# Down projection of a two-layer encoder trunk: the running sums of its weight blocks, added by GpSimd or added by the DMA engines while they load

## The chip, the cores and the metric

The kernel runs on one core of one Trainium2 chip. The metric is the device time of one execution in microseconds, as the median of several runs. Profiles are taken by the hardware profiler from one further execution. The core has TensorE (PE; its weight loads are listed as PEld), VectorE (DVE), ScalarE (ACT), GpSimd (POOL) and SyncE (SP), each with a queue of its own that it works through in order, and sixteen DMA engines that carry the transfers that SP, ACT and POOL issue.

## What is computed

Two batches (512 and 256 tokens, 1024 features) go through a trunk of two layers with shared weights: attention, then a squared-ReLU MLP, each added to the residual stream. Only the last part matters here, once in each layer:

```python
h = rmsnorm(x, ln_mlp[layer])
x = x + jnp.square(jax.nn.relu(h @ w_up[layer])) @ w_down[layer]
```

`w_up` is 1024 x 4096 and `w_down` 4096 x 1024. After the second layer a final RMSNorm gives the output.

## The kernel before

All 768 tokens are kept together, features on the 128 partitions. A product in float32 is made of three passes of reduced precision: each operand is split into a high half and a low half (ACT copies the high half, `whi` or the first plane of `th`; DVE subtracts it to get the low half, `wlo` or the second plane of `th`), and PE adds high x high, high x low and low x high.

Both MLP products are done as 2 x 2 blocks with a scheme of seven block products in place of eight. In such a scheme the operands of the products are sums and differences of the blocks. For the up projection the weights' sums are made on POOL (line 843). The hidden activations, squared, and the differences of them that the down projection needs, go out to DRAM (tensor `T`: ACT's queue stores z, line 879, POOL's queue stores t, line 887) and come back later.

The down projection (from line 953) works through 28 steps in each layer: seven products in the order 1, 2, 7, 4, 5, 6, 3, and in each the four groups `i` of hidden features. A step multiplies 48 times: four banks of 384 columns (`dn`, line 1019), four slices each, three passes each. Its weights are two tiles of 128 x 1024 (`rp` 0 and 1); the first serves the first two banks, the second the last two, so I call the work on one tile a half-step. The weights of a product are:

- product 1: block 11 as loaded; product 7: that tile plus block 21 ("the chain's tile": what product 1 used is added to)
- product 2: block 12 alone
- product 4: block 22, loaded afresh; product 5: that plus block 21; product 6: that plus block 11; product 3: that plus block 12

The host has arranged blocks and signs so that only additions are left. Eight chain tiles are alive (`kept[i, rp]`), and each is split into `whi` and `wlo` (four buffers each) for every product that uses it, then changed in place by the next sum, four steps later (eight steps between products 1 and 7).

Three helpers order the work around step `s`. `fetch(s + 3)` issues the loads of a step's two weight tiles from SP (line 978). They go to `ch` (8 buffers, the chain's tiles), to `wd` (6 buffers) or, every third of the others, to `wraw` (3 buffers, shared with the other stages), as do the two first tiles of all. `sums(s + 2)` adds the loaded block onto the chain's tile on POOL (line 985). `halves(s + 1)` splits (lines 80 and 81). `operand(s + 2)` loads the activations `tr` from `T` through SP (line 911; 768 KB) and splits them into `th` (lines 116 and 117). The framework places all semaphores and plans the order on each engine's queue by its own expected times, so that loads can be issued earlier than the source has them.

At the end of each product DVE adds the banks into the residual x (line 865 through `fold`), ACT evacuates product 1's banks into `u` (line 1025). In layer 1 the final norm is worked in between the last steps (lines 1075 to 1091). When a stage begins, the tiles `ch`, `wd` and `acs` take the places of the up projection's tiles, so their first loads wait until these are free.

Of the kernel before, what the change touches and what calls it, by code (L numbers as in the profile page):

```python
# [11 lines left out]
F32 = mybir.dt.float32  # L12
F32R = mybir.dt.float32r
AF = mybir.ActivationFunctionType
ALU = mybir.AluOpType
AX = mybir.AxisListType

P = 128
# [19 lines left out]
def kernel(ctx: ExitStack, tc: tile.TileContext, a: dict, y: bass.AP):  # L38
    nc = tc.nc
# [3 lines left out]
    wpool = ctx.enter_context(tc.tile_pool(name="wpool", bufs=1))  # L43
# [17 lines left out]
    def ps_tile(tag, name):  # L61
        return psum.tile([P, 512], F32, tag=tag, name=name, bufs=BANKS[tag])
# [706 lines left out]
    def mlp(layer, src, o, x, es):  # L769
# [50 lines left out]
        def weights(plain=False):  # L820


            raws = []
            for _ in range(2):
                raw, loads = wload("w_up", 1024)
                loads[0]()
                raws.append(raw)
            a11, a22, a12, a21 = (r[:, i * 512 : (i + 1) * 512] for r in raws for i in range(2))
            if plain:
                out = {}  # L830
                for t, ij in zip(raws, (((0, 0), (1, 1)), ((0, 1), (1, 0)))):
                    hi, lo = whilo(1024)
                    wsplit(hi, lo, t)
                    for i, b in enumerate(ij):
                        out[b] = (hi, lo), i * 512
                return out
            sa, sb = (up.tile([P, 1024], F32, tag="s", name="s", bufs=3) for _ in range(2))
            s2, s1, s3, s4 = (r[:, i * 512 : (i + 1) * 512] for r in (sa, sb) for i in range(2))
            out = {}
            for ps_, t in (((1, 4), raws[0]), ((6, 5), sa), ((7, 3), sb), ((2,), raws[1])):  # L840
                if t is sa:
                    for d_, x_, y_ in ((s1, a21, a22), (s2, s1, a11), (s3, a11, a21), (s4, a12, s2)):
                        nc.gpsimd.tensor_tensor(out=d_, in0=x_, in1=y_, op=ALU.add)  # L843
                w = 512 * len(ps_)
                hi, lo = whilo(w)
                wsplit(hi, lo, t[:, :w])
                for i, p in enumerate(ps_):
                    out[p] = (hi, lo), i * 512
            return out
# [58 lines left out]
        def operand(n, i):  # L908

            tr = pa_.tile([P, ND, HT], F32, tag="tr", name="tr", bufs=2)  # L910
            nc.sync.dma_start(tr, T[i][:, SLOT[n]])
            th = pa_.tile([P, 2, ND, HT], F32R, tag="th", name="th", bufs=3)
            halve(th[:, 0], th[:, 1], tr)
            return th

        for mp in range(2, FF // 256):
            w = weights()
# [35 lines left out]
        acs = st.enter_context(tc.tile_pool(name="acs", bufs=1, reuse_waits="tile"))  # L953
        wds = ExitStack()
        ch = wds.enter_context(tc.tile_pool(name="ch", bufs=8, side="right", reuse_waits="tile"))
        wd = wds.enter_context(tc.tile_pool(name="wd", bufs=6, side="right", reuse_waits="tile"))
        u = acs.tile([P, 4, HT], F32, name=f"u_{layer}")
        PR = (0, 1)
        ORDER = (1, 2, 7, 4, 5, 6, 3)
# [1 line left out]
        BLOCK = {1: 11, 2: 12, 7: 21, 4: 22, 5: 21, 6: 11, 3: 12}  # L961
        steps = [(n, i) for n in ORDER for i in range(NG)]
        kept, new, parts = {}, {}, {}
        third = [0]

        def fetch(n, i):

            for rp in PR:
                off = (((layer * NG + i) * 4 + (11, 22, 21, 12).index(BLOCK[n])) * 2 + rp) * P * 1024
                if n in (1, 4) and (n, i) != (1, 0):  # L970
                    t = ch.tile([P, 1024], F32, tag="ch", name="ch", bufs=8)
                else:
                    third[0] += n != 1
                    if n == 1 or third[0] % 3 == 0:
                        t = wpool.tile([P, 1024], F32, tag="wraw", name="wd", bufs=3)
                    else:
                        t = wd.tile([P, 1024], F32, tag="wd", name="wd", bufs=6)
                nc.sync.dma_start(t, a["w_down"][off : off + P * 1024].rearrange("(p w) -> p w", w=1024))
                (kept if n in (1, 4) else new)[i, rp] = t

        def sums(n, i):
            for rp in PR:
                if n in (7, 5, 6, 3):
                    t = kept[i, rp]
                    nc.gpsimd.tensor_tensor(out=t, in0=t, in1=new.pop((i, rp)), op=ALU.add)  # L985

        def halves(n, i):
            for rp in PR:
                hi, lo = whilo(1024)
                wsplit(hi, lo, new.pop((i, rp)) if n == 2 else kept[i, rp])  # L990
                parts[n, i, rp] = hi, lo

        def fold(out, x_, op=ALU.add):
            add(out, out, x_, op)
# [7 lines left out]
        for s, (n, i) in enumerate(steps):  # L1002
            if s + 3 < len(steps):
                fetch(*steps[s + 3])
            if s + 2 < len(steps):
                sums(*steps[s + 2])
                ths.append(operand(*steps[s + 2]))
            if s + 1 < len(steps):
                halves(*steps[s + 1])
            if i == 0:  # L1010
                odd = ORDER.index(n) % 2
                banks = [ps_tile("at" if odd or r == 3 else "mm", "dn")[:, :HT] for r in range(4)]
            th = ths.pop(0)
            for r, ps in enumerate(banks):
                w = parts[n, i, r // 2]
                for q in range(ND):
                    c = (r % 2) * 512 + q * P
                    for k, (a_, b_) in enumerate(((0, 0), (0, 1), (1, 0))):
                        nc.tensor.matmul(ps, w[a_][:, c : c + P], th[:, b_, q],  # L1019
                                         start=i + q + k == 0, stop=i == NG - 1 and q == ND - 1 and k == 2)  # L1020
            if i == NG - 1:
                for r, ps in enumerate(banks):
                    x12, x11, x22, x21 = (xb(r, m_, sl) for m_ in PR for sl in (A, B))
                    if n == 1:
                        nc.scalar.activation(u[:, r], ps, AF.Copy)
                    if n in (1, 2):
                        fold(x11, ps)
                    if n == 4:
                        fold(x21, ps)
                    if n in (7, 5):  # L1030
                        fold(x22, ps, ALU.subtract)
                    if n == 7:
                        fold(x21, ps, ALU.subtract)
                    if n in (5, 3):
                        fold(x12, ps)
                    if n == 6:
                        fold(u[:, r], ps)
                        fold(x21, u[:, r], ALU.subtract)
                        fold(x22, u[:, r], ALU.subtract)
                        fold(x12, u[:, r])  # L1040
            if layer == 1 and n == 3 and i < NG - 1:
                last[0](i)
            elif layer == 1 and n == 6 and i == NG - 1:
                last = [final(x, lambda: acs.tile([P, HT], F32, tag="sq", name="sq", bufs=4), s_) for s_ in (HT, 0)]
# [18 lines left out]
    def final(x, sq, s):  # L1063

        acc = cpool.tile([P, NT], F32, tag="acc", name="acc", bufs=1) if s else accs[0]
        R = cpool.tile([P, NT], F32, tag="R", name="R", bufs=1) if s else accs[1]
        accs[:] = [acc, R]
        ms = (0, 2, 4, 6, 1, 3, 5, 7) if s else (1, 3, 5, 7, 0, 2, 4, 6)
        sl = slice(s, s + HT)
        nm = Norm(None, (s, s + HT), acc)  # L1070
        rt = []

        def part(i):
            if i == 0:
                nc.scalar.activation(acc[:, sl], x[ms[0]][:, sl], AF.Square)
                nm.parts = [acc[:, sl]]
                for n, m in enumerate(ms[1:]):
                    t = sq()
                    nc.scalar.activation(t, x[m][:, sl], AF.Square)
                    if n < 5:  # L1080
                        nc.vector.tensor_tensor(out=acc[:, sl], in0=acc[:, sl], in1=t, op=ALU.add)
                    else:
                        nm.parts.append(t)
            elif i == 1:
                rt.append(nm.rstd(s))
            else:
                nm.spread(rt[0], R)
                for k in ms:
                    yt = x[k][:, sl]
                    nc.vector.scalar_tensor_tensor(out=yt, in0=yt, scalar=gcol(G_F, k), in1=R[:, sl], op0=ALU.mult, op1=ALU.mult)  # L1090
                    (nc.sync, nc.scalar)[k // 2 % 2].dma_start(y[:, k, sl], yt)

        return part
# [146 lines left out]
```

## Time and profile before

| | |
|---|---|
| median of 3 runs | 1790.25 us (1785.74 to 1792.01) |
| profiled execution, its time | 1793.21 us |
| profiled execution, its span | 1791.2 us |
| mean granted TensorE clock | 0.982 |
| down projection, layer 0 | about 632 to 876 us of the span |
| down projection, layer 1 | about 1532 to 1777 us of the span |

The span runs from the first to the last instruction of the profiled execution. A group of the profile stands for one line, engine and operation; "idle before" is time in which that engine did nothing just before these instructions. Idle time of an engine that another one covers costs nothing. Busy time of matmuls overlaps between neighbours, so a busy PE says that PE doesn't wait, not that it is at its peak. Not every matmul is recorded.

### The profile page before, as it was taken

Reading aid. Unit: us, or ns where it says so; the run is one execution under the profiler, and the core shown is the slowest. Engines: PE = TensorE matmul, PEld = TensorE weight load, DVE = VectorE, ACT = ScalarE, POOL = GpSimd, SP = SyncE. Lnnn points to the kernel's source line nnn. Section 1 sums busy time; section 2 is a strip of 40 time slices with the busy share of each in tenths; the row PEclk is TensorE's granted clock in tenths of the full one; section 3 lists DMA queues with packets and bytes.
Section 4 is the critical chain, followed back from the end, with each engine's and each line's share of the span. In section 5 each row is a group of like instructions: output and inputs, shape, how many; then the busy total and the mean of one; then the engine's idle time right before and its main releaser. Section 6 shows DMA issues by size and latency. Waiting matters only on the chain.

```text
span 1791.2 us, 28400 instructions
## 1 busy us (share of the span) xinstructions
PE 1728.0 (96%) x10994; PEld 1644.2 (92%) x10994; DVE 1385.5 (77%) x2182; ACT 827.2 (46%) x1509; POOL 583.7 (33%) x456
## 2 busy tenths in 40 slices
PE   7999999998999999999999999999988999999997
PEld 7887888898999989999999999988988999899997
DVE  7777746597888867799656767776878888787995
ACT  6665544363333444444435555554633334444441
POOL 2321000023555404475021212220225554053750
PEclk8999999999999999999999999999999999999998
DMA  5111223312554587664311101112125545977621
GB/s 173 41 33 37 68 71 104 121 48 72 189 163 164 182 329 294 245 204 158 97 46 48 48 25 45 54 57 95 48 69 180 166 166 170 337 271 258 223 89 71
DMA packets 74598, 235.42 MB, mean 131 GB/s; under 512 B 7904, under 2 KB 25056, under 8 KB 74464
## 3 DMA queue, kind: packets, MB, share of 16 engines
q1 hardware_dynamic: 52480, 186.93, 31.1%
q0 software_dynamic: 7168, 25.17, 3.8%
q10 hardware_dynamic: 14816, 21.52, 3.3%
q8 instruction: 86, 1.41, 0.3%
q14 instruction: 48, 0.39, 0.1%
HBM read 182.47 MB, written 50.33 MB: 130 GB/s over the span
## 4 chain that ended last, share of the span: by engine, by line
PE 79%; DVE 10%; issue 4%; ACT 3%; POOL 2%; DMA 2%; POOLq 0%; DVEq 0%; SPq 0%; ACTq 0%
PE dn L1019 26%; PE up L857 18%; PE dqk L190 8%; PE opa L202 5%; PE dvp L190 4%; PE opb L202 2%; PE npa L202 2%; PE ds L268 2%; PE dpv L716 2%; DVE t L792 2%; DVE wlo L81 1%; PE qp L190 1%; PE vp L190 1%; PE npv L596 1%; PE npb L202 1%
## 5 line engine op out<-in xcount | busy, mean ns | idle before, releaser
L857 PE MATMUL up<-c,whi 128*128 128x384 f32 x1824 | 472.8, 341 | 3.0 <-DVE z L865 3.0
L1019 PE MATMUL dn<-th,whi 128*128 128x384 f32 x1792 | 464.6, 340 | 8.4 <-DVE th L117 5.7
L857 PEld LDWEIGHTS up<-c,whi 128*128 128x128 f32 x1824 | 335.6, 191 | 3.7 <-issue 3.6
L1019 PEld LDWEIGHTS dn<-th,whi 128*128 128x128 f32 x1792 | 328.4, 189 | 9.7 <-DVE th L117 6.3
L857 PE MATMUL up<-c,wlo 128*128 128x384 f32 x912 | 311.0, 342 | 13.3 <-DVE wlo L81 13.1
L1019 PE MATMUL dn<-th,wlo 128*128 128x384 f32 x896 | 304.4, 340 | 0.0
L985 POOL TENSOR_TENSOR ch<-ch,wd 128x1024 f32<-128x1024 f32 x60 | 190.7, 3189 | 127.6 <-DVE wlo L81 97.4
L843 POOL TENSOR_TENSOR s<-wraw 128x512 f32<-128x512 f32 x56 | 91.7, 1652 | 368.8 <-DMA wraw<-in_w_up_dram 284.9
L81 DVE TENSOR_TENSOR wlo<-ch,whi 128x1024 fp32r<-128x1024 f32 x88 | 165.7, 1894 | 36.6 <-ACT whi L80 35.1
L857 PEld LDWEIGHTS up<-c,wlo 128*128 128x128 f32 x912 | 173.9, 191 | 15.4 <-DVE wlo L81 15.4
L80 ACT ACTIVATE whi<-ch 128x1024 fp32r<-128x1024 f32 x88 | 93.4, 1064 | 184.7 <-PE dn L1019 147.1
L1019 PEld LDWEIGHTS dn<-th,wlo 128*128 128x128 f32 x896 | 169.7, 189 | 0.0
L81 DVE TENSOR_TENSOR wlo<-wraw,whi 128x1024 fp32r<-128x1024 f32 (+3 forms) x132 | 146.7, 1114 | 27.5 <-ACT whi L80 27.1
L80 ACT ACTIVATE whi<-wraw 128x1024 fp32r<-128x1024 f32 (+3 forms) x128 | 117.0, 916 | 91.6 <-PE up L857 42.7
L117 DVE TENSOR_TENSOR th<-tr,th 128x1536 fp32r<-128x1536 f32 x56 | 131.3, 2347 | 7.6 <-ACT th L116 7.0
L190 PE MATMUL dqk<-whi,xh 128*128 128x256 f32 x384 | 115.9, 302 | 3.1 <-ACT dv L646 3.1
L190 PE MATMUL dqk<-whi,xl 128*128 128x256 f32 x384 | 108.5, 283 | 0.0
L190 PE MATMUL dqk<-wlo,xh 128*128 128x256 f32 x384 | 108.3, 282 | 0.0
L701 ACT ACTIVATE de<-ds,m 128x512 f32<-128x512 f32 (+1 forms) x96 | 58.3, 612 | 81.7 <-DVE m L699 81.7
L878 ACT ACTIVATE z<-z 128x1536 f32<-128x1536 f32 x32 | 47.7, 1490 | 103.0 <-DVE z L876 103.0
L865 DVE TENSOR_TENSOR z<-up,z 128x384 f32<-128x384 f32 x168 | 92.4, 551 | 2.6 <-issue 1.3
L80 ACT ACTIVATE whi<-s 128x1024 fp32r<-128x1024 f32 x56 | 59.5, 1064 | 67.0 <-PE up L857 67.0
(217 smaller groups left out, 3784.4 us busy)
## 6 DMA issues: line engine op xcount, KB each, us to landing
wd<-in_w_down_dram SPq DMA_DIRECT2D x84, 512.0 KB, 4.1
tr<-T SPq DMA_DIRECT2D x56, 768.0 KB, 5.4
wraw<-in_w_up_dram SPq DMA_DIRECT2D x64, 512.0 KB, 3.6
T<-t POOLq DMA_DIRECT2D x64, 384.0 KB, 3.1
T<-z ACTq DMA_DIRECT2D x32, 576.0 KB, 3.0
ch<-in_w_down_dram SPq DMA_DIRECT2D x28, 512.0 KB, 6.0
wraw<-in_w_in_o_dram SPq DMA_DIRECT2D x24, 512.0 KB, 3.6
wraw<-in_w_in_e_dram SPq DMA_DIRECT2D x16, 512.0 KB, 3.6
```

The source lines that it names most:

```text
L80: nc.scalar.activation(hi, raw, AF.Copy)
L81: nc.vector.tensor_tensor(out=lo, in0=raw, in1=hi.bitcast(F32), op=ALU.subtract)
L117: nc.vector.tensor_tensor(out=lo, in0=src, in1=hi.bitcast(F32), op=ALU.subtract)
L190: nc.tensor.matmul(ps[:, :256], st[:, tk], col(k, part, 0, 256), start=(k == 0 and i == 0), stop=(k == KD - 1 and i == 2))
L202: nc.tensor.matmul(ps[:, : e - s], w, mv[:, s:e], start=(k == 0 and i == 0), stop=(k == nk - 1 and i == 2))
L701: nc.scalar.activation(e, s, AF.Exp, bias=m, scale=1.0, accum_out=l2[:, c : c + 1])
L843: nc.gpsimd.tensor_tensor(out=d_, in0=x_, in1=y_, op=ALU.add)
L857: nc.tensor.matmul(ps, part[a_][:, base + k * P : base + (k + 1) * P], t[:, b_], start=start and k + i == 0, stop=stop and k == 3 and i == 2)
L865: nc.vector.tensor_tensor(out=out, in0=x_, in1=y_, op=op)
L878: nc.scalar.activation(z, z, AF.Square)
L985: nc.gpsimd.tensor_tensor(out=t, in0=t, in1=new.pop((i, rp)), op=ALU.add)
L1019: nc.tensor.matmul(ps, w[a_][:, c : c + P], th[:, b_, q], start=i + q + k == 0, stop=i == NG - 1 and q == ND - 1 and k == 2)
```

## The change

The additions of `sums` are gone. Where a block has to be added to a chain's tile (products 7, 5, 6 and 3), `fetch` now issues one transfer from POOL's queue that reads the block in DRAM and adds it onto the tile in SBUF. Loads of products 1, 2 and 4 stay on SP. Since the added blocks need no tile of their own, `wd` serves product 2 alone and has 5 buffers, and `wraw` holds only the first two tiles of product 1. The addition is now issued by the same call as the load before, three steps ahead, and not two.

```diff
-        wd = wds.enter_context(tc.tile_pool(name="wd", bufs=6, side="right", reuse_waits="tile"))
+        wd = wds.enter_context(tc.tile_pool(name="wd", bufs=5, side="right", reuse_waits="tile"))
...
-        third = [0]
...
-                if n in (1, 4) and (n, i) != (1, 0):
-                    t = ch.tile([P, 1024], F32, tag="ch", name="ch", bufs=8)
+                src_ = a["w_down"][off : off + P * 1024].rearrange("(p w) -> p w", w=1024)
+                if n in (7, 5, 6, 3):
+                    nc.gpsimd.dma_start(kept[i, rp], src_, accum_op=ALU.add)
+                    continue
+                if n == 2:
+                    t = new[i, rp] = wd.tile([P, 1024], F32, tag="wd", name="wd", bufs=5)
+                elif i == 0 and n == 1:
+                    t = kept[i, rp] = wpool.tile([P, 1024], F32, tag="wraw", name="wd", bufs=3)
                 else:
-                    third[0] += n != 1
-                    if n == 1 or third[0] % 3 == 0:
-                        t = wpool.tile([P, 1024], F32, tag="wraw", name="wd", bufs=3)
-                    else:
-                        t = wd.tile([P, 1024], F32, tag="wd", name="wd", bufs=6)
-                nc.sync.dma_start(t, a["w_down"][off : off + P * 1024].rearrange("(p w) -> p w", w=1024))
-                (kept if n in (1, 4) else new)[i, rp] = t
-
-        def sums(n, i):
-            for rp in PR:
-                if n in (7, 5, 6, 3):
-                    t = kept[i, rp]
-                    nc.gpsimd.tensor_tensor(out=t, in0=t, in1=new.pop((i, rp)), op=ALU.add)
+                    t = kept[i, rp] = ch.tile([P, 1024], F32, tag="ch", name="ch", bufs=8)
+                nc.sync.dma_start(t, src_)
...
             if s + 2 < len(steps):
-                sums(*steps[s + 2])
                 ths.append(operand(*steps[s + 2]))
```

## The prediction

> **What bounds the kernel now.** I read the page first: the engines' busy time, the chain that ended last, and the group that the change removes.
>
> ```profile
> PE 1728.0 (96%) x10994; PEld 1644.2 (92%) x10994; DVE 1385.5 (77%) x2182; ACT 827.2 (46%) x1509; POOL 583.7 (33%) x456
> PE 79%; DVE 10%; issue 4%; ACT 3%; POOL 2%; DMA 2%; POOLq 0%; DVEq 0%; SPq 0%; ACTq 0%
> L985 POOL TENSOR_TENSOR ch<-ch,wd 128x1024 f32<-128x1024 f32 x60 | 190.7, 3189 | 127.6 <-DVE wlo L81 97.4
> ```
>
> The 60 additions (and four more on wd tiles) are 190.7 us of POOL, but POOL holds 2% of the chain. So the question is what the two stages of the down projection wait for. The windows view cuts them up (its columns: window, length, busy us and count of PE, PEld, DVE, ACT, POOL, granted clock, DMA share, GB/s); the critical view of layer 0 and PE's waits between 600 and 880 us follow.
>
> ```profile
> 600.00:637.50 37.50, 33.34 (x190) 32.69 (x188) 32.82 (x41) 14.71 (x15) 10.25 (x9) 0.98 0.67 236
> ...
> 637.50:680.00 42.50, 42.47 (x227) 42.47 (x228) 29.03 (x24) 21.21 (x21) 5.98 (x4) 0.93 0.85 315
> 680.00:720.00 40.00, 40.00 (x229) 40.00 (x228) 30.36 (x19) 16.66 (x15) 19.98 (x7) 1.00 0.81 302
> 720.00:760.00 40.00, 40.00 (x229) 40.00 (x228) 31.24 (x22) 17.12 (x15) 18.55 (x7) 1.00 0.65 225
> ...
> 800.00:840.00 40.00, 40.00 (x229) 40.00 (x228) 40.00 (x27) 17.80 (x16) 28.60 (x9) 1.00 0.44 139
> ...
> 1500.00:1540.00 40.00, 35.81 (x198) 35.16 (x197) 34.57 (x41) 17.86 (x17) 10.20 (x9) 0.97 0.71 245
> ...
> 1700.00:1740.00 40.00, 40.00 (x230) 40.00 (x229) 40.00 (x29) 17.05 (x16) 27.88 (x8) 1.00 0.31 102
> 1740.00:1777.00 37.00, 37.00 (x221) 37.00 (x220) 24.29 (x39) 12.24 (x16) 1.79 (x1) 1.00 0.13 50
> ```
>
> ```profile
> 637.53 238.64 PE dn L1019 x1340
> ...
> PE dn L1019 <- DVE th L117: 2.8, 1, 2.8
> PE dn L1019 <- DVE z L865: 1.4, 1, 1.4
> ```
>
> The reader should see three things. PE is busy in 40.00 of 40.00 us in every window inside both stages, at a granted clock of 1.00 after the first; the chain runs 238.64 us through L1019 without a break. DVE is full too (40.00 of 40.00 at 800 to 840 and 1700 to 1740), and PE still does not wait: that load lies in slack. And 40 us hold the same 229 recorded matmuls whether POOL works 18.55 or 28.60 us and DMA moves 139 or 302 GB/s, so no relief of POOL speeds up a matmul. What idles PE is only the start of a stage: 2.8 + 1.4 = 4.2 us in layer 0, 40.00 - 35.81 = 4.2 us in layer 1, and a lower clock behind it (0.93 over 42.5 us is 3.0 us lost; 0.97 over 40 us is 1.2).
>
> **What goes.** The additions, and what they slow down. One tile's view gives the sizes (minimum/median/maximum in ns):
>
> ```profile
> L81 DVE TENSOR_TENSOR wlo<-ch,whi x88: 1211/1226/3447, 639.9 to 1759.7; 128x1024 fp32r<-128x1024 f32 x88
> L117 DVE TENSOR_TENSOR th<-tr,th x56: 1745/1759/3970, 635.7 to 1751.8; 128x1536 fp32r<-128x1536 f32 x56
> ...
> L887 POOL DMA_DIRECT2D T<-t x64: 725/725/935, 443.5 to 1542.0; - x64
> SPq L978 <- POOL ch L985: 129.8, 36, 4.7
> ```
>
> POOL loses 64 additions of about 3.19 us, 204 us in all, and gains 64 issues. No accumulating issue is in this trace; the nearest is POOL's own store of t, 0.725 us, so 46 us. DVE's L81 on ch, 165.7 us for 88 by the page's groups, would come to 88 x 1.226 = 108 us if none were slow: 58 us less. All of this is worth 0 us on the path, because PE covers it in every window; without that cover, a DVE full for 80 us in a row would be the bound, which is the state the change takes away. SP loses 64 of its 112 weight issues and the 129.8 us of waits for POOL; behind those waits stand the tr loads, which were never late for PE. Worth 0.
>
> **What comes: the price of an accumulating transfer.** The same 32 blocks per layer come from DRAM, 512 KB each, but each one now also reads its tile in SBUF. From the page's queues and issues:
>
> ```profile
> q1 hardware_dynamic: 52480, 186.93, 31.1%
> wd<-in_w_down_dram SPq DMA_DIRECT2D x84, 512.0 KB, 4.1
> tr<-T SPq DMA_DIRECT2D x56, 768.0 KB, 5.4
> ```
>
> Queue 1 moved 186.93 MB in 31.1% of 1791.2 us = 557 us of all sixteen engines: 336 GB/s. A plain 512 KB is then 1.56 us of the engines, a tr of 768 KB 2.34 us. Lower bound of an accumulation: 1.56 us, since the bytes from DRAM are the same, so no gain in transfers. Upper bound: three one-way transfers of that size (in from DRAM, tile out, tile back), 4.68 us. I take two, 3.12 us: the written side is as before, the read side has doubled, which is nearest to queue 1's row taken twice. The Trainium skill's "Collectives: The Full Stack", section on the bandwidth ceiling, speaks against the change in the same sense: an adding transfer reads two sources over one ring, and it measured 62.28 against 32.35 GB/s. By that the estimate would be 1.93 x 1.56 = 3.0 us and the sum below the same; no run here shows it yet.
>
> **Does it fit?** The pitch and the slack come from layer 0's timeline of ACT and DVE:
>
> ```profile
> 669.06 1.06 ACT L80 ACTIVATE whi<-wd 128x1024 fp32r<-128x1024 f32 x1 [1.41 <-PE dn L1019]
> 690.18 1.06 ACT L80 ACTIVATE whi<-wd 128x1024 fp32r<-128x1024 f32 x1 [3.16 <-PE dn L1019]
> 778.93 1.07 ACT L80 ACTIVATE whi<-ch 128x1024 fp32r<-128x1024 f32 x1 [1.78 <-issue]
> 812.73 1.07 ACT L80 ACTIVATE whi<-ch 128x1024 fp32r<-128x1024 f32 x1 [1.79 <-POOL ch L985]
> ...
> 670.16 2.76 DVE L81 TENSOR_TENSOR wlo<-wd,whi 128x1024 fp32r<-128x1024 f32 x1 [0.62 <-ACT whi L80]
> 781.66 4.56 DVE L81 TENSOR_TENSOR wlo<-ch,whi 128x1024 fp32r<-128x1024 f32 x2
> ```
>
> From 778.93 to 812.73 lie eight half-steps (one tile each): 33.8 / 8 = 4.22 us. The tile split at 778.93 is read for the last time before 781.66 + 4.56 = 786.22 and is needed again at 812.73: at least 26.5 us in which the accumulation must be issued and land. The split itself runs ahead: with four whi buffers a tile copied when its slot frees is multiplied three half-steps later, 12.7 us, of which 786.22 - 778.93 = 7.3 at most go to the split, so 5.4 us more. Latency, from the view of the wd tiles:
>
> ```profile
> DMA to landing us min/median/max: 3.4/4.1/10.4
> ```
>
> Even two of the longest one after the other, 20.8 us, are under 26.5.
>
> Throughput is tightest in products 5, 6 and 3, 24 accumulations in 24 half-steps. Each half-step needs 3.12 + 2.34 / 2 = 4.29 us of the engines against 4.22: 0.07 x 24 = 1.7 us behind at the end, against 31.9 us (26.5 + 5.4) of slack. PE sees nothing. In products 1, 2, 7 and 4 the traffic is higher now (share 0.85 and 0.81), but it is prefetch: product 7's accumulations may start when product 1's tiles are split and are needed 16 half-steps, 68 us, later.
>
> **The new waits.** POOL's issue waits for the split's last read of its tile; behind it stand only further accumulations, and the next stage's small power operation much later. ACT's copy whi now waits for a landing in place of POOL; behind it on ACT stand th's copy and u's evacuations, which PE needs, but only after 26.5 us are used up. Product 2 has five wd slots: tile six of it (copied at 690.18) must wait until the first (copied at 669.06) is read at 670.16 + 2.76 = 672.92, and has 17.3 us to land, more than 10.4.
>
> **Start and end.** Before the stage SP issues three w_down loads and then tr, and DVE finishes z ahead of th's low half:
>
> ```profile
> 606.72 14.57 SPq L978 DMA_DIRECT2D wd<-in_w_down_dram  x3
> 621.33 1.61 SPq L911 DMA_DIRECT2D tr<-T  x2
> ...
> 634.05 1.76 DVE L876 SCALAR_TENSOR_TENSOR z<-z,R 128x1536 f32<-128x1536 f32 x1
> 635.73 3.42 DVE L117 TENSOR_TENSOR th<-tr,th 128x1536 fp32r<-128x1536 f32 x2
> ```
>
> The third of these loads was product 2's tile in wraw, and it has no place there now. But th stands behind z on DVE, and z follows PE, so an earlier tr doesn't move it unless the order on DVE changes. I take 0. After 1740 us DVE has 24.29 of 37.00 busy, so the tail behind the last matmul is not late either: 0. The sum is 0 us: **1790.0 us**, beside a median of 1790.25 (the profiled execution took 1793.21 with a span of 1791.2; no change there is also the claim).
>
> **Rivals.**
>
> A. The DMA engines become the bound, and it is slower. Place: products 5, 6, 3 of each layer. The slack is used up when an accumulation takes (101.3 + 31.9) / 24 - 1.17 = 4.38 us, 2.8 plain loads. At the upper bound of 4.68 us: (4.68 + 1.17 - 4.22) x 24 = 39 us behind, less 31.9 is 7 us a layer, and one stretch of low clock of 3 us each: 20 us in all, 1810. For it: shares of 0.65 already, and GpSimd's queue shares the engines with tr. Against: it takes nearly three transfers' time for one. Chance 0.15.
>
> B. The start of the stage closes up, because with one load fewer and other slots the order on DVE puts th before z. At most 4.2 + 3.0 and 4.2 + 1.2, 12.6 us: 1777. Against: PE also waited 1.4 us for z itself, so moving th ahead moves z back. Chance 0.12, two thirds of it beyond 5 us.
>
> C. The reverse: slots or transfers at the start move the other way, one more gap of the same size in each layer: 1803. Chance 0.08.
>
> D. The change doesn't take the work off POOL: its issues are as long as the additions. Then all is as before, 1790. Chance 0.03, within the same.
>
> Forecast, 0.62.
>
> **Chances and range.** A measurement here can tell 0.3%, 5.4 us, from no change. Faster is B beyond it, 0.08, and 0.02 from the forecast's edge; slower is A 0.14, C 0.07 and 0.02 of the edge; the rest is the same. The range reaches over A's upper bound and most of B and C: 1779 to 1811.
>
> **What would show it.** Right: L1019 idle only at the start, POOL busy down by some 200 us with issues near 0.7 us, L81 near 1.23 us, no window with DVE full, DMA share in products 5, 6 and 3 of 0.8 to 1.0, landings under 26 us. Wrong: waits of ACT's whi for the accumulations that come through to PE in products 5, 6 and 3 (A), or another gap at the start (B, C).

## The result, and the profile after

The changed kernel takes 1803.49 us in the median (1802.04 to 1805.78), the kernel before beside it 1790.01 us: a ratio of 1.008 (95% interval 1.0058 to 1.0101). It is slower by about 13.5 us. The profiled execution has a span of 1803.7 us, 12.5 us more than before. Every median below is one of fast runs: a single execution of e6 at a lower clock (1888.68 us at 0.843) is left out, with which its median would be 1777.80.

The page of the changed kernel first: engines, chain, the two shared queues, and three groups.

```profile
PE 1732.9 (96%) x10994; PEld 1647.5 (91%) x10994; DVE 1277.1 (71%) x2182; ACT 827.3 (46%) x1509; POOL 435.8 (24%) x456
...
q1 hardware_dynamic: 43264, 153.37, 25.3%
q0 software_dynamic: 16384, 58.73, 14.5%
...
PE 75%; DVE 11%; DMA 5%; issue 4%; ACT 3%; POOL 2%; DVEq 0%; POOLq 0%; ACTq 0%; SPq 0%
...
L81 DVE TENSOR_TENSOR wlo<-ch,whi 128x1024 fp32r<-128x1024 f32 x88 | 107.6, 1223 | 111.9 <-ACT whi L80 111.9
...
L971 POOL DMA_DIRECT2D ch<-in_w_down_dram x60 | 51.0, 849 | 337.5 <-DVE wlo L81 333.5
...
L116 ACT ACTIVATE th<-tr 128x1536 fp32r<-128x1536 f32 x56 | 82.8, 1478 | 42.0 <-DMA tr<-T 37.5
```

The relief came: POOL lost 148 us, DVE 108 us, and L81 on the chain's tiles fell from 1894 to 1223 ns. It bought nothing. DMA, 2% of the chain before, is 5% now, and the last row says where: ACT waited 37.5 us for tr. The waits views (total us, times, longest us) compare that with the kernel before, first; the second view is the changed kernel's, with what PE waited for between 640 and 690 us:

```profile
ACT th L116 <- DMA tr<-T: 5.8, 4, 2.8
```

```profile
ACT th L116 <- DMA tr<-T: 37.5, 8, 13.1
...
PE dn L1012 <- ACT th L116: 3.0, 1, 3.0
PE dn L1012 <- DVE th L117: 1.7, 2, 1.1
```

The windows view of the changed kernel shows when (columns as in the prediction: PE, PEld, DVE, ACT, POOL, granted clock, DMA share, GB/s).

```profile
640.00:680.00 40.00, 35.33 (x186) 34.29 (x186) 15.26 (x14) 13.06 (x13) 5.87 (x7) 0.93 1.00 312
680.00:720.00 40.00, 40.00 (x222) 40.00 (x221) 26.40 (x25) 19.12 (x19) 0.00 (x0) 0.96 0.63 218
720.00:760.00 40.00, 40.00 (x229) 40.00 (x229) 23.48 (x23) 16.47 (x14) 5.09 (x6) 1.00 0.84 214
760.00:800.00 40.00, 40.00 (x229) 40.00 (x228) 20.93 (x19) 16.77 (x15) 7.63 (x9) 1.00 1.00 220
...
1540.00:1580.00 40.00, 35.84 (x189) 35.48 (x189) 16.90 (x15) 13.15 (x12) 6.63 (x8) 0.92 1.04 329
1580.00:1620.00 40.00, 38.64 (x204) 38.44 (x204) 27.78 (x27) 21.99 (x24) 0.00 (x0) 0.91 0.55 195
```

In the first 45 us of layer 0's stage PE idles 40.00 - 35.33 = 4.7 us more, all of it (3.0 + 1.7) for th; layer 1 does much the same, the DMA engines are full, and the granted clock falls a second time after the idling. From 760 to 800 us, where the accumulations of products 5 and 6 go out, the engines are full as well, and PE does not miss anything. Full engines alone are not the trouble.

The chain of layer 0 by time (start, length, what; steps of 0.02 to 0.04 us left out), then the issues on POOL, SP and ACT's copy of th, all of the changed kernel:

```profile
636.37 16.36 DMA tr<-T
...
652.75 1.50 ACT th L116
...
654.28 1.77 DVE th L117
...
656.07 18.44 DMA tr<-T
...
674.53 1.49 ACT th L116
...
676.05 1.77 DVE th L117
...
677.86 205.09 PE dn L1012 x1151
```

```profile
627.41 0.94 POOL L971 DMA_DIRECT2D wd<-in_w_down_dram  x1 [0.89 <-DVE wlo L81]
629.55 0.87 POOL L971 DMA_DIRECT2D wd<-in_w_down_dram  x1 [1.20 <-DVE wlo L81]
...
661.20 0.85 POOL L971 DMA_DIRECT2D ch<-in_w_down_dram  x1 [2.89 <-DVE wlo L81]
737.58 0.84 POOL L971 DMA_DIRECT2D ch<-in_w_down_dram  x1 [75.53 <-DVE wlo L81]
...
656.07 0.33 SPq L911 DMA_DIRECT2D tr<-T  x1
...
674.53 1.48 ACT L116 ACTIVATE th<-tr 128x1536 fp32r<-128x1536 f32 x1 [13.10 <-DMA tr<-T]
```

The reader is to see the order of events. POOL issues an accumulation of product 7 as soon as a tile of product 1 has been split: all eight lie between 627 and 661 us, and then nothing for 75 us. The same list of ACT has the first copy of product 7 at 701 us. Meanwhile tr, which is needed at once, takes 16.4 and 18.4 us to land, against a median of 5.4 and a longest of 9.7 before.

### The profile page after: what moved, and what is told of

Read it like the earlier page. It is cut to its first block, busy times and chain, and to the rows that moved or that the text cites. A ratio compares the mean times of both kernels' runs of the same rounds, so it can differ in the third digit from the quotient of the medians.

```text
span 1803.7 us, 28313 instructions
## 1 busy us (share of the span) xinstructions
PE 1732.9 (96%) x10994; PEld 1647.5 (91%) x10994; DVE 1277.1 (71%) x2182; ACT 827.3 (46%) x1509; POOL 435.8 (24%) x456
## 3 DMA queue, kind: packets, MB, share of 16 engines
q0 software_dynamic: 16384, 58.73, 14.5%
## 4 chain that ended last, share of the span: by engine, by line
PE 75%; DVE 11%; DMA 5%; issue 4%; ACT 3%; POOL 2%; DVEq 0%; POOLq 0%; ACTq 0%; SPq 0%
PE dn L1012 22%; PE up L857 17%; PE dqk L190 8%; PE opa L202 5%; PE dvp L190 4%; DMA tr<-T 4%; PE opb L202 2%; PE npa L202 2%; PE ds L268 2%; PE dpv L716 2%; DVE t L792 2%; DVE wlo L81 2%; PE vp L190 1%; DVE z L865 1%; PE qp L190 1%
## 5 line engine op out<-in xcount | busy, mean ns | idle before, releaser
L1012 PE MATMUL dn<-th,whi 128*128 128x384 f32 x1792 | 470.2, 343 | 17.2 <-DVE th L117 8.7
L1012 PEld LDWEIGHTS dn<-th,whi 128*128 128x128 f32 x1792 | 332.2, 191 | 20.1 <-DVE th L117 10.4
L81 DVE TENSOR_TENSOR wlo<-ch,whi 128x1024 fp32r<-128x1024 f32 x88 | 107.6, 1223 | 111.9 <-ACT whi L80 111.9
L81 DVE TENSOR_TENSOR wlo<-wraw,whi 128x1024 fp32r<-128x1024 f32 (+3 forms) x132 | 148.1, 1124 | 29.1 <-ACT whi L80 28.9
L971 POOL DMA_DIRECT2D ch<-in_w_down_dram x60 | 51.0, 849 | 337.5 <-DVE wlo L81 333.5
L117 DVE TENSOR_TENSOR th<-tr,th 128x1536 fp32r<-128x1536 f32 x56 | 98.2, 1756 | 41.8 <-ACT th L116 40.9
L116 ACT ACTIVATE th<-tr 128x1536 fp32r<-128x1536 f32 x56 | 82.8, 1478 | 42.0 <-DMA tr<-T 37.5
```

The lines of the kernel that those rows point to most:

```text
L81: nc.vector.tensor_tensor(out=lo, in0=raw, in1=hi.bitcast(F32), op=ALU.subtract)
L116: nc.scalar.activation(hi, src, AF.Copy)
L117: nc.vector.tensor_tensor(out=lo, in0=src, in1=hi.bitcast(F32), op=ALU.subtract)
L971: nc.gpsimd.dma_start(kept[i, rp], src_, accum_op=ALU.add)
L1012: nc.tensor.matmul(ps, w[a_][:, c : c + P], th[:, b_, q], start=i + q + k == 0, stop=i == NG - 1 and q == ND - 1 and k == 2)
```

## The experiments

The theories: **A**, product 7's early accumulations take the DMA engines from tr; **B**, the engines are too full in products 5, 6 and 3; **C**, the new slots of product 2 changed the order of SP's loads. Later two more were needed, P and G. Each ratio is to runs of the kernel before that were taken beside it.

| run | median us | ratio to before, 95% interval |
|---|---|---|
| e1, product 7 on POOL | 1787.86 | 0.9994 (0.9984 to 1.0003) |
| e2, product 7 alone accumulates | 1801.33 | 1.0070 (1.0055 to 1.0085) |
| e3, product 7 held back | 1781.83 | 0.9953 (0.9936 to 0.9969) |
| e4, plain loads from POOL's queue | 1789.53 | 0.9999 (0.9989 to 1.0009) |
| e6, before, moved by 96 bytes | 1776.67 | 0.9935 (0.9918 to 0.9952) |
| e7, after, moved by 96 bytes | 1794.95 | 1.0039 (1.0024 to 1.0053) |
| e8, held back, nothing moved | 1789.48 | 1.0007 (0.9998 to 1.0016) |
| e9, before, moved by 32 bytes | 1783.07 | 0.9966 (0.9955 to 0.9978) |
| e10, before, moved by 64 bytes | 1782.74 | 0.9963 (0.9950 to 0.9977) |
| e11, before, moved by 128 bytes | 1780.17 | 0.9951 (0.9935 to 0.9967) |
| e12, products 5, 6, 3 accumulate, moved by 96 | 1780.00 | 0.9947 (0.9931 to 0.9963) |
| e13, before, one more write, nothing moved | 1788.07 | 0.9997 (0.9987 to 1.0006) |

### Which accumulations cost: e1 and e2

```diff
-                if n in (7, 5, 6, 3):
+                if n in (5, 6, 3):      # e1; e2: n in (7,)
                     nc.gpsimd.dma_start(kept[i, rp], src_, accum_op=ALU.add)
...
+        def sums(n, i):
+            for rp in PR:
+                if n in (7,):           # e1; e2: n in (5, 6, 3)
+                    t = kept[i, rp]
+                    nc.gpsimd.tensor_tensor(out=t, in0=t, in1=new.pop((i, rp)), op=ALU.add)
```

> Product 7's blocks are loaded by SP and added on POOL as before the change; products 5, 6 and 3 accumulate. Theory A (product 7's eight accumulations are issued some 60 us ahead of need, right at the start of the stage, and take the DMA engines from the tr loads, so that PE waits for th): about 1790 us, no PE idle after the first 5 us of the stage. Theory B (the engines are too full in products 5, 6 and 3): still about 1803. Theory C (the new slots of product 2 changed SP's order and that delays tr): 1790, since the slots are the old ones here; the next runs tell it from A.

> The complement: product 7 accumulates, products 5, 6 and 3 are loaded by SP and added on POOL; product 2 has its old slots (six of wd, every third in wraw). Theory A: about 1803, with tr landings of 15 us or more and PE gaps of 4 to 5 us some 20 to 45 us into each stage. Theories B and C: about 1790.

Windows of e1, two of them:

```profile
640.00:680.00 40.00, 40.00 (x222) 40.00 (x221) 25.60 (x22) 18.32 (x18) 4.92 (x4) 0.97 0.80 300
...
760.00:800.00 40.00, 40.00 (x229) 40.00 (x228) 21.64 (x18) 15.49 (x14) 8.57 (x10) 1.00 1.00 219
```

The same stretch in e2:

```profile
640.00:680.00 40.00, 36.24 (x192) 35.42 (x191) 16.43 (x14) 15.02 (x16) 5.70 (x7) 0.94 1.03 329
```

Twenty-four of a layer's thirty-two accumulations cost nothing, though they fill the engines (1.00); the other eight, alone and with product 2's old slots, cost 12 us over both layers. B falls with e1. C falls with e2, where product 2 has its old slots and the loss is there all the same.

### Price or earliness: e3, e4 and e8

e3 adds, ahead of each accumulation of product 7, two columns that depend on the activations of product 2's step:

```diff
+                    if n == 7:
+                        late = spool.tile([P, 2], F32, tag="late", name="late", bufs=2)
+                        nc.gpsimd.tensor_tensor(out=late, in0=thd[2, i][:, 0, 0, :2].bitcast(F32), in1=nil, op=ALU.mult)
+                        nc.gpsimd.tensor_tensor(out=t[:, :2], in0=t[:, :2], in1=late, op=ALU.add)
                     nc.gpsimd.dma_start(t, src_, accum_op=ALU.add)
```

> The changed kernel, but product 7's accumulations wait on POOL's queue for the activations of product 2's step of the same group (a 128x2 product with zeros of that th is added onto the tile first), so that they come some 30 us later and one step at a time. Theory A: about 1790, PE gaps after the first 5 us of a stage gone, longest tr landing near 10 us. Theories B and C: about 1803.

e4 drops `accum_op=ALU.add` from the four products' transfers, so that their sums are left out.

> The changed kernel with plain loads in place of the accumulations, from the same queue at the same places: the sums of products 7, 5, 6 and 3 are left out (each uses its last block alone). Theory A with the doubled price as its cause: a transfer costs the engines about 1.6 us in place of 3.0, so the eight of product 7 hold them 12 us less, and the time is within 3 us of 1790. If the queue and the early issue alone do it, whatever the price: about 1803.

e4 came out at 1789.53: the same queue, the same places, and half the price, and the stall is gone. Its queue 0 (14.5% in the changed kernel) and the waits of ACT for tr (37.5, 8, 13.1 there):

```profile
q0 software_dynamic: 16384, 58.73, 9.5%
...
ACT th L116 <- DMA tr<-T: 13.0, 6, 3.5
```

Queue 0 also carries the stores of t, 3.8% of 1791.2 us before = 68.1 us, taken as the same in each run. So 64 accumulations take 14.5% of 1803.7 less 68.1 = 193 us of the sixteen engines, 3.02 us each; 64 plain loads take 9.5% of the span of 1785.1 less 68.1 = 101 us, 1.59 us each. The ratio is 1.90. The Trainium skill's page "Collectives: The Full Stack" ("The bandwidth ceiling: the fold count and why AG ≠ RS ≠ AR") has 1.93 between the measured rates of a copying and an adding collective (AllGather and ReduceScatter); the trace agrees.

e3 was 8 us faster than theory A had said, and faster than the kernel before. Holding back had to be tried without what else e3 changes: its two new small tiles (three buffers) move th, and c1 to c3 of the up projection, by 96 bytes. e8 holds back in the same way with an existing tile:

```diff
-                        late = spool.tile([P, 2], F32, tag="late", name="late", bufs=2)
-                        nc.gpsimd.tensor_tensor(out=late, in0=thd[2, i][:, 0, 0, :2].bitcast(F32), in1=nil, op=ALU.mult)
+                        late = spool.tile([P, TT], F32, tag="ms", name="late", bufs=2)[:, :2]
+                        nc.gpsimd.tensor_tensor(out=late, in0=th_, in1=th_, op=ALU.subtract)
```

> Product 7 held back as before, but with the two small columns in a tile that is there anyway (the difference of th with itself in place of the product with zeros), so that no address moves. Theory P with theory A: about 1790, equal to the kernel before, no PE gap after the start of a stage, 176.0 ns a matmul. Theory G: 1782.

Windows of e8, then its waits of ACT for tr:

```profile
640.00:680.00 40.00, 40.00 (x227) 40.00 (x227) 22.53 (x19) 18.90 (x19) 12.52 (x19) 0.99 0.86 278
680.00:720.00 40.00, 40.00 (x229) 40.00 (x229) 22.68 (x19) 16.71 (x15) 3.97 (x6) 1.00 0.93 279
```

```profile
ACT th L116 <- DMA tr<-T: 16.7, 5, 7.2
```

All thirty-two accumulations are back, only eight of them later (they leave from 663 to 685 us in place of 627 to 661); the DMA share is spread (0.86 and 0.93 in place of 1.00 and 0.63), tr is still late, by 7.2 us at most in place of 13.1, and that fits in the slack. The single landing is no shorter: the longest of tr is 20.5 us here and 19.6 in e3, where I had expected some 10, and 21.0 in the changed kernel. What differs is the lead. In the changed kernel the tr load of product 2's first step left at 656.07 us, 17 us before PE ran out of work (its high half was ready at 676.02, and PE had waited 3.0 for it). In e8 the load that took longest in layer 0, 19.2 us for product 7's first step, left at 675.49, some 30 us before that step began (an estimate from the pitch of 4.22 us a half-step). The time is that of the kernel before. This is theory A's core: neither the price nor the early issue is harmful alone, both together are.

### Why e3 was faster: e6, e7, e9 to e13

Two theories. P: the addresses of th and c matter to the matmuls. G: holding back is itself worth 7 us (e8, held back and no faster than the kernel before, speaks against it already).

```diff
+        nil = spool.tile([P, 2], F32, tag="nil", name="nil", bufs=1)
+        nc.vector.memset(nil, 0.0)
+        late = spool.tile([P, 2], F32, tag="late", name="late", bufs=2)
+        nc.vector.memset(late, 0.0)
```

> The kernel before, unchanged but for three unused small tiles of 32 bytes per partition in the pool of statistics, as the held-back run had them: they move th, and c1 to c3 of the up projection, by 96 bytes. Theory P (the held-back run was faster than before because its matmuls read th and c from other addresses: 173.3 ns a matmul in place of 176.0): about 1780, 233 recorded matmuls in 40 us of the down projection in place of 229. Theory G (holding product 7 back is itself worth 7 us): 1789, 229 matmuls.

> The changed kernel with the same three small tiles and nothing held back. Theory P with theory A: the stalls stay and the matmuls are faster, about 1794. Theory G: 1803.

> The kernel before with one small tile, which moves th and c1 to c3 by 32 bytes. th starts at byte 109952 before, a multiple of 128; the up projection's c4 to c7, whose matmuls take 173.3 ns in every run, start 96 bytes past one. Theory P leaves open which part of the address counts: 1780 if any start but a multiple of 128 will do, 1789 if not. Theory G: 1789.

> The kernel before with th and c1 to c3 moved by 64 bytes. Moved by 32, th's matmuls took 173.3 ns and those of c1 to c3 still 176; moved by 96, both 173.3. If only a start at a multiple of 128 bytes is slow for th: th 173.3 ns and a time of 1778 to 1784, by what c1 to c3 do. If 64 is as bad as 0: 176.0 and 1789.

> The kernel before with th and c1 to c3 moved by 128 bytes, so that they start at multiples of 128 again. If the address modulo 128 is what counts: 176.0 ns and 1789 again. If any move away from the old place helps: 173.3 ns and about 1778.

> The kernel before with the same extra write of a small tile by DVE as in the moved kernels, but into a tile that is there anyway, so that no address moves. If the addresses made the moved kernels faster: 176.0 ns a matmul of the down projection and 1789. If the extra instruction did (another order or alignment of the queues): 173.3 ns and about 1780.

e9 and e11 have only the first of the two tiles, with one and four buffers, e10 with two; e13 writes into a tile of the pool that is there anyway. One window each, of e6, of e11 and of e13:

```profile
720.00:760.00 40.00, 40.00 (x233) 40.00 (x232) 34.83 (x23) 17.24 (x15) 22.95 (x8) 1.00 0.62 222
```

```profile
720.00:760.00 40.00, 40.00 (x233) 40.00 (x232) 32.84 (x22) 17.34 (x15) 20.95 (x8) 1.00 0.67 245
```

```profile
720.00:760.00 40.00, 40.00 (x229) 40.00 (x229) 31.88 (x22) 16.73 (x15) 19.16 (x7) 1.00 0.67 237
```

With PE busy for all 40.00 us at a clock of 1.00, e6 and e11 show 233 matmuls where e13 and the kernel before show 229. From start to start, as a mean over all recorded neighbours of the trace, a matmul of the down projection takes 176.0 ns in the kernel before and after e13's write, 173.3 ns moved by 32, 96 or 128 bytes, 174.7 ns moved by 64, which neither side of e10's expectation had. Over the 2688 matmuls of the two stages 2.7 ns are 7 us; those of the up projection, 174.8 ns in the mean before and 173.4 in e6, give some 4 more, and that is about what e6 gained. So the place decides and not the extra instruction, and G falls. My guess that only starts at multiples of 128 bytes are slow falls with e11. And e9 shows that one rule for all tiles is too simple: th was faster there, while part of the matmuls of the up projection kept 176 to 177 ns. What in the addresses it is stays open.

e7 gives the change once more at the faster place: 1794.95 against 1776.67 of e6, 18 us slower. The stall is there whatever the pace.

### Is the relief of POOL and DVE worth anything: e12

The edit is e1's together with the two tiles above.

> Product 7 added on POOL, products 5, 6 and 3 accumulated, and everything moved by 96 bytes. If the freed POOL and DVE are worth something once the matmuls are faster: clearly under the 1777.8 us of the kernel before moved by 96. If PE covers them still: 1778, equal to it.

e12 and e6 can't be told apart (1780.00 and 1776.67, ratios whose intervals overlap). At the faster pace too PE covers the additions. The fastest kernel of the study is the kernel before with th and c moved: 0.9935, without any accumulation.

## Why the prediction was wrong, point by point

**What bounds the kernel**: right. PE was the bound, and the relief of POOL and DVE was worth nothing: e8, with all the additions gone and no stall, takes the time of the kernel before, and e1 and e12, with three quarters of them gone, say the same. DVE lost 108 us where I had counted 58 for L81, since L117 fell too, from 131.3 to 98.2 us.

**The price of an accumulation**: right. I took 3.12 us of the engines for 512 KB, measured were 3.02. POOL's issue took 0.85 us where I had 0.725.

**Products 5, 6 and 3**: right. I had 4.29 us of work for the engines in a half-step of 4.22 and no loss; the engines were full (shares of 0.97 to 1.00 from 760 to 840 us) and PE lost nothing. Rival A, placed there, did not happen.

**Product 7, the step that failed**: "In products 1, 2, 7 and 4 the traffic is higher now (share 0.85 and 0.81), but it is prefetch". That overlap was put at nothing. I asked whether the accumulations would be in time, and they were: the last landed at 673.33 us and its tile was copied at 730.74, 57 us later. I didn't ask what stood beside them. Eight of them are 8 x 3.02 = 24 us of work for engines that were busy to 0.83 in the kernel before (640 to 680 us, below), with the first of product 7's plain loads among that, and nothing but the split holds them back. The tr loads need the engines just then; before they were waited for 2.8 us at most, now 13.1, and PE idled 4.7 us in layer 0 and 4.3 in layer 1 that the prediction had put at 0. What I wrote of the tr loads behind SP's waits, that they were "never late for PE", was true of a trace in which the blocks had to wait for free tiles on SP (four loads leave from 672.95 us on, the first of them when product 2's first tile had been read, at 672.92), and that brake went with the change.

**The new waits**: the landing was off, the conclusion right. Product 2's tiles took up to 23.2 us to land, where the longest so far was 10.4; ACT waited for them twice, 4.1 us in all, and in both stages PE waited only for th and, at the start, for z.

**The lower clock**: I put it into rivals only. The windows view around both starts, of the kernel before and then of the changed one:

```profile
600.00:640.00 40.00, 35.81 (x198) 35.16 (x197) 35.32 (x43) 17.21 (x17) 10.25 (x9) 0.95 0.70 246
640.00:680.00 40.00, 40.00 (x221) 40.00 (x220) 26.53 (x23) 18.71 (x19) 5.98 (x4) 0.96 0.83 310
...
sum 120.00, PE 115.81 PEld 115.16 DVE 92.21 ACT 52.58 POOL 36.21; mean PE 38.60 PEld 38.39 DVE 30.74 ACT 17.53 POOL 12.07
...
1540.00:1580.00 40.00, 40.00 (x227) 40.00 (x226) 27.81 (x22) 18.31 (x18) 7.11 (x5) 0.99 0.85 313
1580.00:1620.00 40.00, 40.00 (x229) 40.00 (x228) 33.60 (x23) 19.30 (x19) 18.09 (x6) 1.00 0.82 297
sum 120.00, PE 115.81 PEld 115.16 DVE 95.98 ACT 55.48 POOL 35.40; mean PE 38.60 PEld 38.39 DVE 31.99 ACT 18.49 POOL 11.80
```

```profile
600.00:640.00 40.00, 35.81 (x194) 35.16 (x194) 35.12 (x43) 17.39 (x17) 12.52 (x11) 0.94 0.75 238
...
sum 120.00, PE 111.14 PEld 109.45 DVE 76.78 ACT 49.57 POOL 18.38; mean PE 37.05 PEld 36.48 DVE 25.59 ACT 16.52 POOL 6.13
...
1500.00:1540.00 40.00, 37.05 (x210) 36.09 (x208) 35.48 (x44) 16.90 (x17) 15.82 (x14) 1.00 0.68 219
...
sum 120.00, PE 111.54 PEld 110.01 DVE 80.16 ACT 52.04 POOL 22.44; mean PE 37.18 PEld 36.67 DVE 26.72 ACT 17.35 POOL 7.48
```

The sums are over 600 to 720 and 1500 to 1620 us. PE idles 4.7 and 4.3 us more, 8.9 together. The clock takes about as much again: 0.94, 0.93 and 0.96 in place of 0.95, 0.96 and 1.00 in the three windows of layer 0, and 1.00, 0.92 and 0.91 in place of 0.97, 0.99 and 1.00 in those of layer 1, or (0.08 + 0.13) x 40 = 8.4 us. The matmuls agree: the six windows hold 97 fewer, which at 229 in 40 us are 17 us. The span grew by 12.5; some 5 us are gained elsewhere, where I have no cause to name, and single executions of the kernel before already differ by 6 us (1785.74 to 1792.01).

**The start of the stage**: right. PE's first 4.2 us of waiting are in every run, with and without the change.

**The rivals**: C named the size (1803) and that another gap would open near the start, and got 0.08. It spoke of slots or transfers that move at the start; the slots are excluded by e2, and it did not see that the change's own transfers would be the cause. That its 1803 is the time measured is in part luck: it had 8.4 us of waiting and 4.2 of clock, and the runs have 8.9 and 8.4, with some 5 gained elsewhere. B did not happen (the start is as it was), nor D (an issue takes 0.85 us, an addition took 3.19).

## What to carry to other kernels

A transfer that waits for nothing but its own tile goes out as soon as it can: when work moves onto the DMA engines, ask for each of their stretches which urgent load would share them, not only whether the new transfer will be in time. An accumulating transfer costs the engines about two plain ones. Here twenty-four a layer were free in products 5, 6 and 3, though they filled the engines, and sixteen in the whole kernel, beside the prefetch at the start of each stage, cost 12 us until something held them back. And when an experiment adds a small tile, look whether it moves the big ones: here 96 bytes gained nearly what the change cost, 12 against 13.5 us, so a control run with the tile alone belongs beside it.

## What the runs showed of the hardware that was not expected

The pace of matmuls depends on where an operand (here th) lies in SBUF, by 1.5% (173.3 against 176.0 ns for 384 columns), with no idle time in any view; it shows in the count of matmuls in a full window and in the time from one start to the next. Which part of the address decides is not shown. A DVE subtraction of two tiles (L81 on ch) took 1.22 us alone and up to 3.45 us beside POOL's additions: in the kernel before all 32 of the 88 that took over 1.3 us ran while an addition did, and with the additions gone the longest was 1.23 us.
